# Down projection as seven block products on one Trainium2 core

## Chip, cores and metric

The kernel runs on one core of one Trainium2 chip, as one program. The metric is the device time of one execution in microseconds (us). Three runs of the kernel before took 3605.74, 3605.95 and 3608.25 us; the median is 3605.95 us.

## What is computed

The reference is a two-block model on a sequence of 2048 tokens and 1024 channels, all in float32. The first block is a state space and pooling mixer followed by a gated feed-forward; the second is banded attention beside a gated linear attention, an output product and a second gate. The part that matters here is the feed-forward of the first block:

```
n2 = rmsnorm(h, norm2_g)
ff = silu(n2 @ w_gate) * (n2 @ w_up)      # 1024 -> 2816 columns
h  = h + ff @ w_down                      # 2816 -> 1024 columns
out = rmsnorm(h, final_norm_g)
```

After it a layer norm feeds the second block. 2816 columns are 22 groups of 128 (NFF), 1024 channels are 8 groups of 128 (KT).

## The kernel before, in words

All float32 products run on TensorE as three products of rounded parts. A number x is split into hi (ScalarE copies it to the rounded type float32r, L54) and lo (x minus hi, on VectorE or GpSimd, L44); then hi*hi, hi*lo and lo*hi are summed in PSUM (`mm3`, L163 to L165). A tile is 128 channels x 512 tokens, so a matmul is 128x128 weights against 128x512 values.

The engines have short names in the profile: PE (TensorE), DVE (VectorE), ACT (ScalarE), POOL (GpSimd), SP (its queue issues all loads; ACT's queue issues all stores). Each engine runs its instructions in a fixed order. The program is written for a tile framework that orders the instructions of all engines ahead of time by a simulated timeline: an instruction that stands early in the text has priority, but one that stands later can go ahead when its inputs are simulated to be ready. A generator `self.bg` holds background work (`bg_step`, L892), which only sets where that work stands in the text.

Tokens come in two halves of 1024, and a half in two blocks of 512. For each half there is a gate stage (`gu_half`, L1082) and a down stage (`down`, L1190).

*Gate stage.* For each j of 22 it makes gate and up products for 128 columns of ff and both token blocks. It does so already by seven block products (Winograd's form of Strassen's scheme): gate and up are the two row blocks, the two token blocks the column blocks, and the two halves of the 1024 inputs the inner blocks. A product is 4 x 3 matmuls, so a j has 84. The sums of the inputs are made once per half (`gu_in`, L983), the sums of the weights for each j (`gu_w`, L1037) with the splits on ACT, DVE and POOL. The results h0 and h1 (one per token block) are split by `put` (L1104) into a hi and a lo tile, hid, and stored to memory (`hid_d`), 512 KB each.

*Down stage.* For each token block the 22 hid tiles are loaded again and multiplied with the 22 weight groups of w_down: per j eight output groups m of three matmuls, all eight PSUM banks in use. The weights are loaded and split (ACT, then POOL) anew for each token block through the ring of `get_w`, 88 times in all. After the last j of a block the eight banks are added to h (DVE, L51), the squares and the weighted sum for the next norms are accumulated on ACT, POOL and DVE, and the result is stored (first half) or kept (second half). While down runs in the first half, `gu_in(1)` prepares the second half's inputs; in the second half `proj_in_steps` (L1240) prepares the next stage's. While the gate stage of the second half runs, `norm(0)` and `norm(1)` (L1251) work on the first half's results.

Names that the change and the prediction touch: `weights` (L112), `mix_out` (L953), `gu_w`, `gu_prime` (L1076), `gu_half`, `put`, `slot` (L1156), `fetch` (L1172), `down`, `norm`, `load_x` (L1350). Tiles by name: wr (raw weights), wh and wl (their hi and lo), wru, wsh, wsl, wth, wtl (further gate weight tiles), xh and xl (inputs), raw, t, s, sq, nh, ls (128x512 work tiles), pa, pb, pc (PSUM banks of the gate stage), dn (those of the down stage). A line in the profile can be that of a helper: L44 is every tensor_tensor, L51 every scalar_tensor_tensor, L54 every ScalarE function, L57 a load and L60 a store.

Of the kernel before, what the change touches and what calls it, by code (L numbers as in the profile page):

```python
# [6 lines left out]
F32 = mybir.dt.float32  # L7
F32R = mybir.dt.float32r
# [5 lines left out]
D = 1024  # L14
# [21 lines left out]
class Build:  # L36
# [75 lines left out]
    def weights(self, stage):  # L112
# [7 lines left out]
        for _ in range(2):  # L120
            for j in range(NFF):
                yield a["w_down"][j], sh, None, None
        if stage == "down0":
            return
        for _ in range(2):
# [51 lines left out]
    def run(self):  # L177
        tc, a = self.tc, self.a
        with ExitStack() as ctx:
            dram = ctx.enter_context(tc.tile_pool(name="dram", bufs=1, space=bass.MemoryType.DRAM))  # L180
            for name, shape, dt in (("u_d", [4, T, 128, NCH], F32), ("yp_d", [512, S], F32), ("ys_d", [4, T, 128, NCR], F32),
                                    ("h1_d", [D, S], F32), ("h2_d", [D, S], F32), ("r2_d", [4, 512], F32), ("ryp_d", [1, S], F32), ("rys_d", [T, NCR], F32),
                                    ("h3_d", [D, S], F32), ("hid_d", [4, NFF, 128, 2, 512], F32),
# [610 lines left out]
    def phase_main(self):  # L794
# [4 lines left out]
        with ExitStack() as ctx:  # L799
# [11 lines left out]
            with tc.tile_pool(name="ffn", bufs=1) as self.fp:  # L811
                self.xr.append(self.fp)
                with tc.tile_pool(name="psf", bufs=8, space=PSUM) as self.ps:
# [16 lines left out]
                    for half in range(2):  # L830
                        self.bg = [self.norm(0), self.norm(1)] if half else [self.bias_table()]
# [8 lines left out]
                    self.bg = [self.norm(2), self.norm(3)]  # L840
# [112 lines left out]
    def mix_out(self, bs, start=(), steps=range(8), last=False):  # L953
        a = self.a
        before, self.r2_todo = self.r2_todo, []
        ss = [self.fp.tile([128, 512], F32, tag="hid" if bs[0] else "st2", name="ss", bufs=2) for _ in bs]
# [26 lines left out]
    def gu_in(self, half):  # L983
# [9 lines left out]
        def fetch(k):  # L993
            out = []
            for n, (kk, i) in enumerate(((k, 0), (k, 1), (k + 4, 0), (k + 4, 1))):
                t0 = half * 1024 + i * 512
                f = self.tmp("s", 2) if n % 2 else self.fp.tile([128, 512], F32, tag="nh", name="nh", bufs=2)
# [39 lines left out]
    def gu_w(self, j):  # L1037


        rg, ru = self.gu_raws  # L1040
        w = self.gw = {}
# [11 lines left out]
        if j + 1 < NFF:  # L1053
            self.gu_raws = [self.gu_load(j + 1, up) for up in (False, True)]
# [21 lines left out]
    def gu_prime(self):  # L1076

        self.gu_raws = [self.gu_load(0, False), None]
        self.gw_steps = self.gu_w(0)
        next(self.gw_steps)  # L1080

    def gu_half(self, half):  # L1082
# [21 lines left out]
        def put(i, h):  # L1104
            x = self.fp.tile([128, 2, 512], F32R, tag="hid", name="hid", bufs=2)
            self.split(x[:, 0], x[:, 1], h)
            self.store(self.hid_d[2 * half + i, j], x.bitcast(F32))

        for j in range(NFF):
            w = self.gw  # L1110
            nw = self.gu_w(j + 1) if j + 1 < NFF else iter(())
# [9 lines left out]
            if j == NFF - 1:  # L1121
                self.w_all = self.weights(f"down{half}")
                self.w_next.append(self.get_w(0))
                self.down_start(half)
                self.fetch()
                self.fetch()
# [14 lines left out]
            if j == NFF - 1:  # L1141
                self.fetch()
                self.fetch()
            self.tt(h1, h1, p5, ALU.mult)
            put(1, h1)
# [5 lines left out]
            self.tt(h0, pa, h0, ALU.mult)  # L1151
            put(0, h0)
# [802 lines left out]
```

## Time and profile before

| | |
|---|---|
| median of three runs | 3605.95 us |
| the profiled execution's own time | 3604.71 us |
| its span, first to last instruction | 3602.7 us |
| mean granted TensorE clock | 0.963 of full speed |
| first gate stage begins | 680 us |
| first down stage begins | 1117 us |
| second gate stage begins | 1386 us |
| second down stage begins, ends | 1843, 2086 us |

The stages overlap a little, since the ordering lets instructions of the next stage run early; the borders are those of the first or last matmul of a stage, within a few us. "Busy" is the time in which an engine had at least one instruction running; matmuls overlap, so a busy PE says that it did not stand still, and the distance between starts says how fast it went. PEclk is the granted clock, 1.00 being 2.4 GHz. An instruction's duration on DVE or POOL contains waits for a place in memory that the two share, if there are any.

### The profile page before, as it was taken

The page shows a single profiled execution, that of the slowest core. Times are in us where ns is not written, and L with a number is a line of the kernel's source. Part 1 is how long each engine was busy: PE and PEld are TensorE (multiplying, and loading weights), DVE is VectorE, ACT ScalarE, POOL GpSimd, SP SyncE. Part 2 cuts the span into 40 slices and gives each one's busy share as a digit, 9 for nine tenths or more (in the row PEclk, how much of TensorE's full clock was granted, in tenths as well). Part 3 has the DMA queues.
Part 4 walks back from the last instruction along what each step waited for, and adds up shares of the span by engine and source line. Part 5 has one row for each costly group of instructions (what it writes and reads, how often), then busy time and mean ns, then how long its engine had stood idle before and what let it go on. Part 6 is the DMA issues. An engine that isn't in the chain of part 4 may idle for free.

```text
span 3602.7 us, 45654 instructions
## 1 busy us (share of the span) xinstructions
PE 3326.9 (92%) x16138; PEld 2761.8 (77%) x16138; DVE 2092.3 (58%) x3365; ACT 1565.5 (43%) x2750; POOL 1569.8 (44%) x1146
## 2 busy tenths in 40 slices
PE   7887788899999999999999989999999999979897
PEld 7676666678887877777777877798888987767676
DVE  7776556766667015777642073235666446787874
ACT  5343533334344223445332132335655445666653
POOL 1265544444454455555445453222322235353544
PEclk9998899899999999999999999999999999989898
DMA  9643376442335564444366535665564665555351
GB/s 252 143 108 102 87 227 189 138 141 100 112 117 187 186 237 152 144 167 157 115 234 208 191 124 172 172 185 173 158 185 135 171 194 148 163 141 159 115 170 49
DMA packets 330268, 568.10 MB, mean 158 GB/s; under 512 B 85004, under 2 KB 171556, under 8 KB 330040
## 3 DMA queue, kind: packets, MB, share of 16 engines
q1 hardware_dynamic: 226944, 419.21, 39.6%
q10 hardware_dynamic: 103096, 145.97, 11.7%
q8 instruction: 128, 2.10, 0.2%
q14 instruction: 100, 0.82, 0.1%
HBM read 409.04 MB, written 145.94 MB: 154 GB/s over the span
## 4 chain that ended last, share of the span: by engine, by line
PE 36%; DVE 7%; DMA 5%; ACT 3%; issue 2%; POOL 1%; SPq 0%; ACTq 0%; DVEq 0%; POOLq 0%
PE pt L165 4%; PE pt L163 4%; PE pt L164 4%; PE pa L1092 3%; PE dn L163 2%; PE dn L164 2%; PE dn L165 2%; PE pv L1562 2%; PE s L1520 1%; PE pv L1391 1%; PE pv L1392 1%; PE pc L1092 1%; PE pv L1390 1%; PE tp L1546 1%; DMA raw<-mix_d 1%
## 5 line engine op out<-in xcount | busy, mean ns | idle before, releaser
L44 POOL TENSOR_TENSOR wl<-wr,wh 128x1024 fp32r<-128x1024 f32 (+1 forms) x235 | 587.2, 2500 | 564.4 <-ACT wh L54 512.0
L54 ACT ACTIVATE wh<-wr 128x1024 fp32r<-128x1024 f32 (+2 forms) x289 | 301.4, 1046 | 497.3 <-PE dn L164 275.7
L163 PE MATMUL pt<-xh,wh 128*128 128x512 f32 x896 | 358.8, 401 | 8.7 <-DVE t L51 4.2
L165 PE MATMUL pt<-xh,wl 128*128 128x512 f32 x896 | 358.2, 400 | 2.1 <-POOL wl L44 1.7
L164 PE MATMUL pt<-xl,wh 128*128 128x512 f32 x896 | 357.7, 399 | 0.0
L163 PE MATMUL dn<-hin,wh 128*128 128x512 f32 x704 | 281.8, 400 | 10.7 <-ACT wh L54 7.5
L164 PE MATMUL dn<-hin,wh 128*128 128x512 f32 x704 | 279.7, 397 | 0.0
L48 POOL TENSOR_SCALAR P<-P,rsm 128x640 f32<-128x640 f32 (+4 forms) x128 | 103.8, 811 | 348.3 <-DVE rsm L1530 285.5
L1092 PE MATMUL pa<-xh,wh 128*128 128x512 f32 x528 | 211.7, 401 | 14.3 <-ACT t L54 9.3
L165 PE MATMUL dn<-hin,wl 128*128 128x512 f32 x704 | 215.3, 394 | 0.0
L1092 PE MATMUL pa<-xh,wl 128*128 128x512 f32 x528 | 207.9, 400 | 2.1 <-POOL wl L44 2.1
L1092 PE MATMUL pa<-xl,wh 128*128 128x512 f32 x528 | 209.8, 397 | 0.0
L44 POOL TENSOR_TENSOR wl<-wru,wh 128x1024 fp32r<-128x1024 f32 x44 | 107.6, 2446 | 234.2 <-ACT wh L54 234.1
L163 PEld LDWEIGHTS pt<-xh,wh 128*128 128x128 f32 x896 | 170.0, 190 | 46.1 <-issue 3.9
L44 POOL TENSOR_TENSOR hid<-raw,hid 128x512 fp32r<-128x512 f32 x88 | 126.8, 1453 | 165.3 <-issue 121.7
L165 PEld LDWEIGHTS pt<-xh,wl 128*128 128x128 f32 x896 | 169.0, 189 | 38.0 <-POOL wl L44 2.4
L164 PEld LDWEIGHTS pt<-xl,wh 128*128 128x128 f32 x896 | 169.3, 189 | 35.0 <-issue 0.7
L51 DVE SCALAR_TENSOR_TENSOR h<-dn,h 128x512 f32<-128x512 f32 x32 | 19.8, 678 | 267.2 <-PE dn L165 182.3
L163 PEld LDWEIGHTS dn<-hin,wh 128*128 128x128 f32 x704 | 134.2, 191 | 46.4 <-ACT wh L54 10.9
L1525 DVE CUSTOM_DVE_ANT_0 P<-s,bias 128x640 f32<-128x640 f32 (+4 forms) x128 | 94.5, 738 | 108.5 <-PE s L1520 59.9
L164 PEld LDWEIGHTS dn<-hin,wh 128*128 128x128 f32 x704 | 134.3, 191 | 29.9
L1390 PE MATMUL pv<-wh,xh 128*128 128x256 f32 (+1 forms) x512 | 148.7, 294 | 8.8 <-ACT wh L54 5.4
(474 smaller groups left out, 9345.8 us busy)
## 6 DMA issues: line engine op xcount, KB each, us to landing
hid_d<-hid ACTq DMA_DIRECT2D x88, 512.0 KB, 3.5
wr<-in_w_down SPq DMA_DIRECT2D x88, 512.0 KB, 3.5
hin<-hid_d SPq DMA_DIRECT2D x88, 512.0 KB, 4.2
wr<-in_w_out SPq DMA_DIRECT2D x56, 512.0 KB, 4.3
wr<-in_w_in SPq DMA_DIRECT2D x44, 512.0 KB, 4.5
wru<-in_w_up SPq DMA_DIRECT2D x44, 512.0 KB, 3.7
wr<-in_w_gate SPq DMA_DIRECT2D x44, 512.0 KB, 3.5
raw<-h_d SPq DMA_DIRECT2D x64, 256.0 KB, 4.0
```

The costliest lines, as they stand in the source:

```text
L44: return (eng or self.dve).tensor_tensor(out=o, in0=x, in1=y, op=op)
L48: (eng or self.dve).tensor_scalar(out=o, in0=x, scalar1=s1, scalar2=s2, op0=op0, **kw)
L54: return self.act.activation(out=o, in_=x, func=func, **kw)
L163: self.pe.matmul(ps, lhsT=hi[k], rhs=xh[k], start=(first and k == 0), stop=False)
L164: self.pe.matmul(ps, lhsT=hi[k], rhs=xl[k], start=False, stop=False)
L165: self.pe.matmul(ps, lhsT=lo[k], rhs=xh[k], start=False, stop=(last and k == n - 1))
L1092: self.pe.matmul(ps, lhsT=l_[:, k], rhs=x[k][r_], start=(first and k == n == 0), stop=(k == 3 and n == 2), skip_group_check=True)
L1390: self.pe.matmul(pt, lhsT=xh, rhs=whi[:, k % 4], start=(k == 0), stop=False)
L1391: self.pe.matmul(pt, lhsT=xh, rhs=wlo[:, k % 4], start=False, stop=False)
L1392: self.pe.matmul(pt, lhsT=xl, rhs=whi[:, k % 4], start=False, stop=(k == KT - 1))
L1525: self.dve.tensor_tensor_reduce(out=v3(P[:, 0:w]), in0=sp[:, 0:np_, 0:n], in1=v3(bias[:, 640 - w:640]), scale=1.0, scalar=3e38, op0=ALU.ad ...
L1562: self.pe.matmul(pv, lhsT=VH[:, kb + x - kt0], rhs=self.PT[m][ch][:, sl], start=(n == 0 and m == 0), stop=(n == len(idxs) - 1 and m == 1))
```

## The change

The down product is made by seven block products too. The 22 groups of ff are taken in two halves of 11 (inner blocks: j and j + 11), the 8 output groups in two halves of four, and the two token blocks of a half are the column blocks. So that j and j + 11 come one after the other, the gate stage goes through the groups in the order 0, 11, 1, 12, ... (`gu_js`). It stores h0 and h1 as they are, and with them three more tiles made of sums on POOL: seven tiles of 256 KB for each pair (`hd_d`). The down weights' four sums (128x512 for each of 11 j) are made once by POOL in the first gate stage, in 44 steps of four operations on 128x128 (`down_sums`, two steps per j), and stored (`sd_d`).

The down stage then has 7 products x 11 j = 77 steps per half. A step loads a 128x512 weight tile and a 128x512 ff tile (`dn_load`), splits both on ACT and DVE (`dn_split`, the subtraction by the default engine of `halves`, DVE), and runs 4 m x 3 matmuls into four banks. The products alternate between two sets of four banks (pa, pb). Some results are copied to SBUF (`hold`); outputs are finished four at a time after products 2, 7, 3 and 4, one per step. `dn_load` runs five steps ahead of the matmuls, `dn_split` two; a step's split tiles come in three sets. Other edits move tiles to other tags (places in memory), and the two norms of a half change their order. Weights of the next stages are requested in step 75 of 77.

```diff
@@ gu_w
+        nxt = self.gu_js[j + 1:j + 2]
+        j = self.gu_js[j]
...
@@ gu_half
-        def put(i, h):
-            x = self.fp.tile([128, 2, 512], F32R, tag="hid", name="hid", bufs=2)
-            self.split(x[:, 0], x[:, 1], h)
-            self.store(self.hid_d[2 * half + i, j], x.bitcast(F32))
+        def keep(name):
+            return self.fp.tile([128, 512], F32, tag=name, name=name, bufs=1)
+        def less(o, x, y):
+            self.tt(o, x, y, ALU.subtract, eng=self.pool)
+        def put(p, x):
+            self.store(self.hd_d[half, p - 1, jj], x)
+        sums = iter(()) if half else self.down_sums()
         for j in range(NFF):
+            jj, late = j // 2, j % 2
             w = self.gw
+            next(sums, None)
...
-            self.tt(h1, h1, p5, ALU.mult)
-            put(1, h1)
+            if late:
+                self.tt(h1, h1, p5, ALU.mult)
+                put(3, h1)
+                less(hb, h1, hb)
+                put(7, hb)
+                less(hc, h1, hc)
+                put(6, hc)
+            else:
+                hb = keep("hb")
+                self.tt(hb, h1, p5, ALU.mult)
+            next(sums, None)
...
-            self.tt(h0, pa, h0, ALU.mult)
-            put(0, h0)
+            if late:
+                self.tt(h0, pa, h0, ALU.mult)
+                put(2, h0)
+                less(ha, h0, hc)
+                put(4, ha)
+            else:
+                ha, hc = keep("ha"), keep("hc")
+                self.tt(ha, pa, h0, ALU.mult)
+                put(1, ha)
+                less(hc, hb, ha)
+                put(5, hc)
...
+    def down_sums(self):
+        wd, h = self.a["w_down"], NFF // 2
+        def fetch(j, m):
+            t = self.fp.tile([128, 4, 128], F32, tag="ls", name="sd", bufs=3)
+            self.load(t[:, 0:2], wd[j][:, m::4])
+            self.load(t[:, 2:4], wd[j + h][:, m::4])
+            return t
...
+            for o, x, y, op in ((1, 0, 1, ALU.subtract), (3, 3, 1, ALU.subtract), (0, 0, 3, ALU.add), (2, 2, 3, ALU.subtract)):
+                self.tt(t[:, o], t[:, x], t[:, y], op, eng=self.pool)
+            self.store(self.sd_d[:, j, :, m * 128:(m + 1) * 128].rearrange("s p c -> p s c"), t)
+            yield 1
...
+        self.dn = [(p, j) for p in (1, 2, 6, 5, 7, 3, 4) for j in range(NFF // 2)]
...
+    def dn_split(self):
...
+        w, x = self.dn_raw.pop(0)
+        if self.dn_s % 3 == 1:
+            wh, wl, xh, xl = (self.fp.tile([128, 512], F32R, tag=t, name=t, bufs=1) for t in ("wth", "wtl", "hc", "hd"))
+        else:
+            h, l_ = (self.wp.tile([128, 2, 512], F32R, tag=t, name=t, bufs=2) for t in ("wh", "wl"))
+            wh, xh, wl, xl = h[:, 0], h[:, 1], l_[:, 0], l_[:, 1]
+        self.halves((wh, wl), w)
+        self.halves((xh, xl), x)
...
@@ down
+        def out(x):
+            o, i, m = h1.pop(0)
+            self.stt(o, x, 0.5, o, ALU.mult, ALU.add)
...
+            self.add_sq(sq, o, first)
...
+                self.stt(sz, o, gf[:, m:m + 1], sz, ALU.mult, ALU.add)
+            if not half:
+                self.store(self.h3_d[m * 128:(m + 1) * 128, b * 512:(b + 1) * 512], o)
+            fetch()
...
+            if p in (1, 6, 5):
+                self.fn(hold[p][m], ps, AF.Copy)
+            elif p == 4:
+                out(ps)
+            else:
+                x = hold[{2: 1, 7: 5, 3: 6}[p]][m]
+                self.tt(x, ps, x, ALU.add)
+                out(x)
...
+        for n, (p, j) in enumerate(self.dn):
+            self.dn_split()
+            self.dn_load()
+            wh, wl, xh, xl = self.dn_ops.pop(0)
+            ps = pa if p in (1, 6, 7, 4) else pb
+            for m in range(4):
+                c = slice(m * 128, m * 128 + 128)
+                for i, (l_, r_) in enumerate(((wh, xh), (wh, xl), (wl, xh))):
+                    self.pe.matmul(ps[m], lhsT=l_[:, c], rhs=r_, start=(p in (1, 2, 5) and j == i == 0),
+                                   stop=(j == NFF // 2 - 1 and i == 2), skip_group_check=True)
+            if post:
+                done(*post.pop(0))
+            if j == NFF // 2 - 1:
+                post += [(p, m) for m in range(4)]
+            if n % 4 == 1:
+                self.bg_step()
```

## Rows read from the trace of the kernel before

**Rows 1.** The page's first part: busy us (share of the span) and instructions.

```profile
PE 3326.9 (92%) x16138; PEld 2761.8 (77%) x16138; DVE 2092.3 (58%) x3365; ACT 1565.5 (43%) x2750; POOL 1569.8 (44%) x1146
```

**Rows 2.** Busy time by stage: stretch, length, busy us (instructions), PEclk, DMA, GB/s.

```profile
680.00:1117.00 437.00, 425.76 (x1814) 343.63 (x1813) 290.22 (x299) 175.94 (x254) 209.13 (x112) 0.99 0.33 116
1117.00:1386.20 269.20, 259.36 (x1094) 208.18 (x1093) 72.72 (x67) 66.91 (x80) 139.46 (x65) 0.98 0.64 213
1386.20:1843.00 456.80, 443.04 (x1881) 355.79 (x1881) 321.58 (x337) 206.82 (x298) 236.11 (x128) 0.99 0.42 145
1843.00:2086.00 243.00, 240.41 (x1036) 194.80 (x1037) 42.36 (x37) 62.10 (x73) 120.05 (x54) 1.00 0.65 218
```

**Rows 3.** Instructions that write the tile dn: ns min/median/max, first and last start.

```profile
L163 PE MATMUL dn<-hin,wh x704: 388/395/797, 1117.3 to 2085.3; 128*128 128x512 f32 x176
```

**Rows 4.** Timeline of PE in the first gate half: start us, us, instruction.

```profile
859.91 0.40 PE L1092 MATMUL pa<-xh,wth 128*128 128x512 f32 x1
...
871.93 0.39 PE L1092 MATMUL pa<-xl,wh 128*128 128x512 f32 x1
```

**Rows 5.** PE's waits, 680 to 2086 us: total us, times, longest.

```profile
PE dn L163 <- ACT wh L54: 7.5, 6, 2.7
...
PE dn L163 <- ACT sq L54: 3.0, 2, 1.5
```

**Rows 6.** Busy time of PE (matmuls) in three stretches, PEclk, DMA, GB/s.

```profile
800.00:1100.00 300.00, 300.00 (x1301) 1.00 0.31 111
1120.00:1180.00 60.00, 53.40 (x208) 0.91 0.67 223
1200.00:1220.00 20.00, 20.00 (x88) 1.00 0.58 186
```

**Rows 7.** Timeline of PE around one stall; in brackets the idle time before.

```profile
1467.91 0.56 PE L1092 MATMUL pa<-xh,wh 128*128 128x512 f32 x1 [4.71 <-ACT t L54]
...
1471.66 0.40 PE L1092 MATMUL pa<-xh,wh 128*128 128x512 f32 x1
```

**Rows 8.** Instructions that write or read hid, 800 to 1100 us.

```profile
L54 ACT ACTIVATE hid<-raw x31: 615/616/634, 800.1 to 1091.7; 128x512 fp32r<-128x512 f32 x31
L44 POOL TENSOR_TENSOR hid<-raw,hid x31: 1278/1297/1767, 802.6 to 1095.0; 128x512 fp32r<-128x512 f32 x31
L60 ACTq DMA_DIRECT2D hid_d<-hid x31: 326/326/327, 804.0 to 1096.7; - x31
```

**Rows 9.** Groups of POOL instructions by form: count, busy us, mean ns, idle before.

```profile
L44 POOL TENSOR_TENSOR ed<-Lc 128x256 f32<-128x256 f32 x16 | 11.6, 723 | 55.8 <-DVE Lc L1659 55.8
...
L44 POOL TENSOR_TENSOR vsq<-vsq 128x128 f32<-128x128 f32 x16 | 9.4, 588 | 0.4
```

**Rows 10.** Timeline of POOL in the first gate half.

```profile
858.47 2.40 POOL L44 TENSOR_TENSOR wl<-wru,wh 128x1024 fp32r<-128x1024 f32 x1 [10.02 <-ACT wh L54]
...
863.80 2.40 POOL L44 TENSOR_TENSOR wl<-wr,wh 128x1024 fp32r<-128x1024 f32 x1
```

**Rows 11.** Timeline of DVE in the first gate half.

```profile
859.71 0.69 DVE L44 TENSOR_TENSOR t<-pb,t 128x512 f32<-128x512 f32 x1 [1.46 <-PE pb L1092]
...
864.03 2.72 DVE L44 TENSOR_TENSOR wtl<-sq,wth 128x512 fp32r<-128x512 f32 x1 [1.34 <-ACT wth L54]
...
868.97 0.68 DVE L44 TENSOR_TENSOR sq<-wru 128x512 f32<-128x512 f32 x1
...
872.53 1.23 DVE L44 TENSOR_TENSOR wsl<-wr,wsh 128x1024 fp32r<-128x1024 f32 x1 [0.17 <-ACT wsh L54]
```

**Rows 12.** Timeline of ACT in the first gate half.

```profile
876.74 1.06 ACT L54 ACTIVATE wh<-wru 128x1024 fp32r<-128x1024 f32 x1 [0.99 <-PE pa L1092]
...
877.71 0.63 ACT L54 ACTIVATE hid<-raw 128x512 fp32r<-128x512 f32 x1
```

**Rows 13.** Groups of DVE instructions by form in the first down half.

```profile
L51 DVE SCALAR_TENSOR_TENSOR s<-h,v_final_norm_g,s 128x512 f32<-128x512 f32 x7 | 12.8, 1832 | 0.2
```

**Rows 14.** Busy time in the first 100 us.

```profile
0.00:100.00 100.00, 78.36 (x426) 75.07 (x426) 79.31 (x330) 50.14 (x92) 17.65 (x43) 0.93 0.91 240
```

More of the change, by code (lines that the diff above doesn't have):

```diff
@@ new lines, in down, with fetch @@
+        for _ in range(3):
+            self.dn_load()
+        self.dn_split()
+        pb, pa = ([self.ps.tile([128, 512], F32, tag="ps", name=n, bufs=8) for _ in range(4)] for n in ("pb", "pa"))
+        outs = [(i, m) for i, m0 in ((0, 0), (1, 4), (1, 0), (0, 4)) for m in range(m0, m0 + 4)]
+        h1, kept, sums, hold, post = [], [[None] * KT for _ in range(2)], {}, {}, []
+        def fetch():
+            if outs:
+                i, m = outs.pop(0)
+                if half:
+                    t = kept[i][m] = self.fp.tile([128, 512], F32, tag="x", name="h3", bufs=20)
+                else:
+                    t = self.fp.tile([128, 512], F32, tag=("ha", "hb")[m % 2], name="h3", bufs=1)
+                b = 2 * half + i
+                self.load(t, self.h1_d[m * 128:(m + 1) * 128, b * 512:(b + 1) * 512])
+                h1.append((t, i, m))
@@ new lines, in out @@
+        def out(x):
+            o, i, m = h1.pop(0)
+            b = 2 * half + i
+            self.stt(o, x, 0.5, o, ALU.mult, ALU.add)
+            first = i not in sums
+            if first:
+                sums[i] = [self.tmp("s", 2) if i else self.fp.tile([128, 512], F32, tag="st2", name="st2", bufs=2)
+                           for _ in range(2)]
+            sq, sz = sums[i]
+            self.add_sq(sq, o, first)
+            if first:
+                self.ts(sz, o, gf[:, m:m + 1], ALU.mult)
+            else:
+                self.stt(sz, o, gf[:, m:m + 1], sz, ALU.mult, ALU.add)
+            if not half:
+                self.store(self.h3_d[m * 128:(m + 1) * 128, b * 512:(b + 1) * 512], o)
+            fetch()
@@ new lines, in places, with done @@
+        def places(p):
+            two = [self.fp.tile([128, 2, 512], F32, tag=t, name="hold", bufs=n)
+                   for t, n in ((("wsh", 1), ("wsl", 1)) if p == 5 else (("wru", 2), ("wru", 2)))]
+            hold[p] = [t[:, e] for t in two for e in range(2)]
+        def done(p, m):
+            ps = (pa if p in (1, 6, 7, 4) else pb)[m]
+            if p in (1, 6, 5):
+                if m == 0:
+                    places(p)
+                self.fn(hold[p][m], ps, AF.Copy)
+            elif p == 4:
+                out(ps)
+            else:
+                x = hold[{2: 1, 7: 5, 3: 6}[p]][m]
+                self.tt(x, ps, x, ALU.add)
+                out(x)
@@ new lines, in down @@
+        for _ in range(2):
+            fetch()
+        for n, (p, j) in enumerate(self.dn):
+            self.dn_split()
+            self.dn_load()
+            wh, wl, xh, xl = self.dn_ops.pop(0)
[11 more added lines that the diff above has]
+                self.bg_step()
+            if n == 75:
+                if half:
+                    self.w_all = self.weights("proj")
+                    self.w_next.append(self.get_w(0))
+                else:
+                    self.gu_prime()
+                    next(self.gw_steps)
@@ L1236, in down @@
+        while post:
+            done(*post.pop(0))
+        self.stats = [(*sums[i], kept[i] if half else []) for i in range(2)]
         if half == 0:
@@ L1267, in tiles @@
             return out
-        for _ in range(3 if b % 2 == 0 else 0):
+        if b % 2:
             yield 1
```

123 lines of the change are left out of this document (40 added, 83 removed).

## The prediction

> **What bounds the kernel now.** I read the page's first part, then busy time by stage, then the down products' own instructions, then PE's waits and 20 us stretches. TensorE is busy 92% of the span [rows 1]. The four stages that the change touches run from 680 to 2086 us, and PE is busy for 425.8 of 437.0, 259.4 of 269.2, 443.0 of 456.8 and 240.4 of 243.0 us there [rows 2]: PE sets the time, and 37 us of idle time stand against it. The reader should see that DVE, ACT and POOL have room in the two down stages (DVE 73 of 269 and 42 of 243 us), less in the gate stages.
>
> The down products are 3 x 704 = 2112 matmuls [rows 3]. One lasts 0.39 us, but they are pipelined, so their price is the distance of starts: 53 starts in a row lie between 859.91 and 871.93 us, so 12.02 / 52 = 0.231 us each [rows 4]. 2112 x 0.231 = 488 us.
>
> Of the idle time, 7.5 us is PE waiting for the down weights' rounding and 3.0 us (two waits) for the square that stands before the release of a bank where one token block's down ends and the next begins [rows 5]. The first costs more than its waits: 208 matmuls run from 1120 to 1180 us where 60 / 0.231 = 260 would fit (1301 do in 300 us of the gate stage), so 52 x 0.231 = 12 us are lost at the start of the first down [rows 6]. A stall also lowers the clock: after a wait of 4.71 us the next nine matmuls take from 1467.91 to 1471.66 us, 3.75 instead of 2.08 us, half the pace [rows 7]. So such a stall costs 4.7 + 1.7 = 6.4 us.
>
> **The change, part by part.** *Matmuls.* A half now takes 7 block products x 11 j x 4 m x 3 = 924 matmuls instead of 1056; over both halves 264 fewer, 264 x 0.231 = 61.0 us, all on PE, the bounding engine: -61.0.
>
> *Gate stage, both halves.* Per j two ScalarE roundings of hid go (0.616 each) and two POOL subtractions stay in number (1.297 each, now between h tiles). ACT-queue stores go from 2 to 3.5 per j at 0.326 us of ACT [rows 8]: ACT gains 1.23 and pays 0.49 us. DVE's count is the same. In the first gate half the two sums stores add 0.65. Taken as 0; ends -3 and +5, since a store now waits at the head of ACT's queue for POOL's subtraction, as it does today for hid.
>
> *Weight sums, first gate half.* 44 steps of four POOL operations on 128x128. The one row of that form means 588 ns; going down from 1.297 us at 512 columns [rows 8] and 0.723 at 256 gives 0.44 [rows 9]. So 176 operations add 77 to 103 us of POOL. Each step also puts two loads on SP's queue (prefetched a step ahead) and a store on ACT's, ahead of the next gate weights and copies.
> POOL alone has room (209 of 437 us, rows 2), but it hinders DVE. A DVE subtraction from two SBUF tiles that starts 0.23 us into a 2.40 us POOL operation lasts 2.72 us, ending 0.55 us after it; one that reads PSUM lasts 0.69 beside the same POOL form [rows 10, 11]. So POOL and DVE's two-SBUF operations take turns. Per j that is on POOL 2 x 2.40 + 3 x 1.30 = 8.7 us and on DVE seven of 0.68 and one of 1.23, 6.0 us [rows 11]: 14.7 of the 84 x 0.231 = 19.4 us that PE takes. With eight sums it is 18.2 to 19.4. If nothing overlapped at all, DVE's four PSUM reads included (2.8 us), it would be 21.0 to 22.2, so 22 x 1.6 to 2.8 = 35 to 62 us late. Lower end 0: in the middle of this stage PE is busy for 300.0 of 300 us [rows 6]. Nearest row for a value: the second gate half has 27.0 us more POOL time than the first and 13.8 instead of 11.2 us of PE idle [rows 2]. 90 / 27.0 x 2.6 = 8.7; I take +8.
> The Trainium skill (SBUF — State Buffer, section "Who interferes with whom") says that a DVE instruction with both inputs in SBUF and a GpSimd one that reads SBUF exclude each other for the whole instruction, and one with a PSUM input does not join in; the rows agree (2.72 against 0.69 us). By it alone the demand just fits, the term is 0 and the sum 8 us lower; it speaks against the place of the sums, not against the change.
>
> *Down stage, splits.* Before, ACT rounds the weights (1.06 for such a tile) and POOL subtracts (2.40) once per 24 matmuls [rows 10, 12], and hid comes split from memory. Now each of the 154 steps of 12 matmuls (12 x 0.231 = 2.77 us) has two ACT roundings (1.23 us) and two DVE subtractions (2 x 0.68 = 1.36 us). Both run beside PE: 44% and 49% of a step. A split's operands come free three steps ahead, so it has two steps, 5.55 us, for a chain of about 0.62 + 0.62 + 0.68 and hand-overs, some 2.6 us: slack 2.9 us. Cost 0 in the steady state. Without this cover, PE would wait for the whole excess of each step.
>
> *Down stage, outputs.* Evacuations are now spread: copies to SBUF after products 1, 6 and 5 (a ScalarE pass as hid's, about 0.62, four each), and four outputs, one per step, after products 2, 7 and 3; the last four come after product 4. The old block switch and its 3.0 us go: -3. An output is a sum, two more DVE operations and a POOL addition. The accumulation of the normalisation's sum means 1.832 us where POOL adds the squares, against 0.68 unhindered [rows 11, 13]. In turns: splits 1.36 + two of 0.68 + 1.30 = 4.0 us against a step of 2.77: 1.25 late per step, 5.0 in four, less the slack of 2.9: 2.1 us of stall, in six bursts (three in each half). Ends: 0 (the order lets the splits go first) and 6 x (4.0 + 1.7) = 34 with the clock's fall. I take 6 x 2 = +12.
>
> *Starts and ends of the down stages.* Step 1's operand lands in the tile hc, which is free only after the last gate product, a DVE multiplication (0.69), a POOL subtraction (1.30) and its store: its split ends 3.5 us or so after the gate stage, PE needs it after 2.77. +1 per half, +2; ends 0 and +14. The background work of the first down (13 DVE operations for each of 4 k, as before) still meets its first steps, so I leave the 12 us lost there as they are; ends -11 and +11. At the end four outputs instead of eight are left, but the next gate's third weight tile must wait for the last step, which uses its place: 0, ends -5 and +5.
>
> *Transfers.* 512 KB per 12 matmuls is as many bytes per matmul as now (512 KB of weights and 512 KB of hid per 24): 524 KB / 2.77 us = 189 GB/s. The down stages move 213 and 218 GB/s at a share of 0.64 and 0.65 [rows 2]. Rows of a transfer get half as long. Five steps are loaded ahead. The nearest stretch with shorter rows moves 240 GB/s at a share of 0.91 [rows 14]; by that the down would need a share of 0.72. Taken as 0. Upper end: part of the six bursts' end above, since a load that is late stops the same split.
>
> **Sum.** The profiled execution took 3604.7 us (span 3602.7 and 2.0 around it). 3604.7 - 61.0 + 8 - 3 + 12 + 2 = 3562.7. The median before is 3605.95, 1.2 above, so 3564.
>
> **Rivals.** (a) Nothing new stalls: the order of the work absorbs sums and bursts, 3606 - 61 - 3 = 3542. For it: the 300 us without a wait. Against it: each of the four stages has some idle time already. (b) The outputs' bursts and late loads stall each time and pull the clock down: 3564 + (34 - 12) = 3586. For it: the 1.832 us; against: only 4 of 11 steps have outputs. (c) Slower: ACT's queue. A sums store stands in ACT's order until POOL's four operations end; behind it stands the copy of pa, without which PE may not add product 6 into that bank. If POOL is late by its turns with DVE, PE stalls as at 1467.91 (6.4 us). Once in every j of the first gate half this is 22 x 6.4 = 141, so 3564 + 141 = 3705. Alone it turns the gain of 42 us into a loss from 42 / 6.4 = 7 such stalls; once in two j gives 3564 + 70 = 3634. For it: that very wait is the one of [rows 7]. Against: ACT's order does not follow the program text in the trace: the rounding of wru runs at 876.74 us, ahead of hid's at 877.71 that stands before it in the text [rows 12]; so a waiting store is placed late; and today's stores wait for POOL in the same way at little cost. (d) The products are not fewer in time: no, 264 matmuls less can't fail to show on PE's count.
>
> **How the numbers follow.** Forecast (3550 to 3580) 0.53, (a) 0.16, (b) 0.16, (c) 0.12, and 0.03 for an even outcome. The range reaches to (a) and past (b) to the even outcome: 3540 to 3606, leaving about 0.15 to 0.2 out. About 0.2% (7 us) can be told from no change here: faster (under 3599) 0.83, same 0.05, slower 0.12.
>
> **What would show it.** Down matmuls 1848, and PE busy less by 264 of them; the two down stages about 30 us shorter each. In the first gate half POOL about 80 to 100 us busier, DVE's two-SBUF means longer, PE idle 8 us more. In the down, PE waits for xl, wl or xh in steps 22 to 26, 55 to 59 and 66 to 70 of each half. Wrong: PE waits for the copy of pa in most j (case c), or no waits at output bursts (case a).

## The result, and the profile after

The changed kernel takes 3578.76 us (median; 3573.63 to 3588.34 in 4 runs) where the kernel before took 3605.84 beside it: a ratio of 0.9927 [0.9904, 0.9951], some 27 us less. The forecast was 3564, 42 us less, with a range of 3540 to 3606. So sign and range held, and a third of the gain is missing. The profiled execution is the longest of the four, 3588.3 us (span 3586.4), 16.4 less than the 3604.7 before. One execution of e2_nosums (4700 us) and one of e7_normsp (9742 us), further down, took far longer than the others of the same kernel and are left out of the medians.

The page's first part answers [rows 1]: 16138 - 15874 = 264 matmuls fewer, as stated, and PE busy 53.1 us less.

```profile
PE 3273.8 (91%) x15874; PEld 2712.4 (76%) x15874; DVE 2253.7 (63%) x3697; ACT 1608.9 (45%) x2906; POOL 1469.1 (41%) x1234
```

The four stages of [rows 2], cut at the first matmul of each (columns as there; the last gate products still run beside the first down step):

```profile
679.20:1135.20 456.00, 431.19 (x1816) 342.80 (x1815) 267.16 (x294) 150.28 (x209) 302.56 (x271) 0.98 0.46 149
1135.20:1376.80 241.60, 225.12 (x961) 183.30 (x960) 168.97 (x242) 116.05 (x205) 46.43 (x23) 0.96 0.69 221
1376.80:1840.90 464.10, 435.94 (x1825) 347.58 (x1824) 314.00 (x334) 182.17 (x255) 230.46 (x124) 0.97 0.40 135
1840.90:2077.70 236.80, 224.18 (x960) 181.69 (x959) 144.81 (x208) 110.50 (x193) 23.24 (x15) 0.97 0.62 198
```

The first gate stage got 18.7 us longer than [rows 2] has it (437.3 from 680.0 to 1117.3), with POOL busy 302.6 instead of 209.1 us. The down stages lost matmuls, but not the 30 us each that 132 fewer should give: from first down matmul to the end, 268.9 became 241.6 and 255.7 (before, from 1829.6 us) became 236.8. PE is idle for 16 and 13 us in them.

What PE waited for, from 680 to 2086 us, answers [rows 5]:

```profile
PE pa L1091 <- ACT t L54: 28.8, 16, 7.9
PE pa L1316 <- ACT hc L54: 20.2, 2, 10.3
PE pa L1091 <- ACT wth L54: 6.7, 1, 6.7
PE pb L1316 <- DVE hd L44: 5.3, 2, 4.3
PE pa L1091 <- DVE wtl L44: 3.8, 1, 3.8
...
PE pc L1091 <- ACT wsh L54: 3.2, 1, 3.2
```

Four things are to be seen there, and each was followed to its place.

*The sums came early.* All instructions on the tile of the weight sums (ns min/median/max, first and last start):

```profile
L44 POOL TENSOR_TENSOR sd<-sd x176: 446/464/1457, 653.5 to 890.0; 128x128 f32<-128x128 f32 x176
...
L60 ACTq DMA_DIRECT2D sd_d<-sd x44: 366/377/711, 657.4 to 890.5; - x44
```

The text asks for two of the 44 steps per j over 22 j, to 1135 us. They ran from 653 to 890 us, in half that time. PE's pace in three stretches (busy us, matmuls, PEclk, DMA, GB/s) shows the price: 797 matmuls from 680 to 900 us, where the kernel before ran 875, and where the pace of [rows 6] (1301 in 300 us) would give 954:

```profile
680.00:900.00 220.00, 195.19 (x797) 0.95 0.66 203
900.00:1140.00 240.00, 240.00 (x1039) 1.00 0.29 101
1225.00:1376.00 151.00, 151.00 (x665) 1.00 0.73 236
```

In the first stretch the stall of rival (c) happened, with the shape that the prediction gave it. The timeline of all engines around the longest wait:

```profile
763.67 2.55 POOL L44 TENSOR_TENSOR sd<-sd 128x128 f32<-128x128 f32 x5
...
765.84 0.38 ACTq L60 DMA_DIRECT2D sd_d<-sd  x1
766.57 0.75 DVE L51 SCALAR_TENSOR_TENSOR nh<-nh,v_norm_g,r 128x512 f32<-128x512 f32 x1 [2.31 <-DMA nh<-h_d]
768.89 0.75 DVE L51 SCALAR_TENSOR_TENSOR nh<-nh,v_norm_g,r 128x512 f32<-128x512 f32 x1 [1.57 <-DMA nh<-h_d]
769.37 1.40 POOL L44 TENSOR_TENSOR sd<-sd 128x128 f32<-128x128 f32 x3 [3.15 <-DMA sd<-in_w_down]
769.56 0.69 DVE L44 TENSOR_TENSOR ha<-pa,raw 128x512 f32<-128x512 f32 x1
770.27 0.34 ACTq L60 DMA_DIRECT2D hd_d<-ha  x1
...
770.80 0.37 ACTq L60 DMA_DIRECT2D sd_d<-sd  x1
771.27 0.63 ACT L54 ACTIVATE wth<-sq 128x512 fp32r<-128x512 f32 x1 [8.58 <-DMA sd_d<-sd]
...
771.81 0.58 ACT L54 ACTIVATE t<-pa 128x512 f32<-128x512 f32 x1
...
772.44 0.80 PE L1091 MATMUL pa<-xh,wh 128*128 128x512 f32 x1 [7.87 <-ACT t L54]
```

ACT does nothing for 8.58 us, from 762.69 us on, and the copy of pa (tile t) behind is what PE wants. Three stores stand at ACT's head in turn. A sums store waits for POOL's sums until 765.84. The store of the gate output ha then waits until 770.27 for DVE, which writes ha at 769.56 and had stood waiting for loads of nh. A second sums store goes at 770.80. So the sums' stores hold ACT for some 3.3 us of the 8.58 and the gate output's store for 4. Such a wait is long only once: of the nine waits for t, 14.1 us in all, one has 7.9 and one 2.5, and the others have 1.1 or less.

*The output bursts cost nothing.* The third stretch above holds all three bursts of the first down half, from 1228 to 1364 us, and PE has no gap in it. The engines do take turns there, as a pair of one burst shows in the timeline:

```profile
1321.66 2.00 POOL L44 TENSOR_TENSOR s<-s,sq 128x512 f32<-128x512 f32 x1 [79.26 <-ACT sq L54]
...
1322.43 1.79 DVE L51 SCALAR_TENSOR_TENSOR s<-h,v_final_norm_g,s 128x512 f32<-128x512 f32 x1
```

The splits are simply not delayed by more than their slack. In the second half PE waits 2.7 us in all between 1880 and 2078 us.

*Each down half starts late.* PE waits 10.31 us in its second step (and 9.93 at 1862 us). The timeline around the tile hc, from the last gate matmul on:

```profile
1146.01 0.40 PE L1091 MATMUL pa<-xh,wl 128*128 128x512 f32 x1
...
1146.59 1.27 POOL L44 TENSOR_TENSOR hb<-raw,hb 128x512 f32<-128x512 f32 x1 [14.37 <-issue]
...
1147.81 1.71 POOL L44 TENSOR_TENSOR hc<-raw,hc 128x512 f32<-128x512 f32 x1
...
1150.89 0.33 ACTq L60 DMA_DIRECT2D hd_d<-hc  x1
...
1156.04 0.63 ACT L54 ACTIVATE hc<-s 128x512 fp32r<-128x512 f32 x1 [0.75 <-DMA hd_d<-hc]
...
1156.72 0.79 PE L1316 MATMUL pa<-hc,wth 128*128 128x512 f32 x1 [10.31 <-ACT hc L54]
```

POOL's result of 1149.5 is stored from 1150.89 on, and the tile is free 5 us later, when the store has landed. Only then may step 1's operand be rounded into it. Most stores of this tile land sooner, and these two land while the DMA engines are full. The landing of all its stores, then the two stretches from issue to reuse (1st and 2nd half; columns as in [rows 2]):

```profile
DMA to landing us min/median/max: 2.0/2.3/5.7
...
1150.89:1156.04 5.15, 0.00 (x0) 0.00 (x0) 5.12 (x7) 3.42 (x6) 2.53 (x3) 0.54 0.99 331
1856.53:1861.41 4.88, 0.00 (x0) 0.00 (x0) 3.28 (x5) 1.77 (x3) 1.15 (x1) 0.50 0.99 322
```

The mean DMA share of the two stages is 0.69 and 0.62. That the full engines make the landing long fits, but no run tests it.

*The second gate half starts late.* The timeline around its third weight tile, wth:

```profile
1379.32 2.03 SPq L57 DMA_DIRECT2D h<-h_d  x2
...
1382.42 0.69 DVE L51 SCALAR_TENSOR_TENSOR h<-pa,h 128x512 f32<-128x512 f32 x1 [1.47 <-DMA h<-h_d]
...
1383.16 5.96 POOL L44 TENSOR_TENSOR st<-st,sq 128x512 f32<-128x512 f32 x4
...
1387.93 1.74 DVE L44 TENSOR_TENSOR sq<-wru 128x512 f32<-128x512 f32 x1
...
1389.70 0.63 ACT L54 ACTIVATE wth<-sq 128x512 fp32r<-128x512 f32 x1 [1.80 <-DVE sq L44]
...
1390.39 0.80 PE L1091 MATMUL pa<-xh,wth 128*128 128x512 f32 x1 [6.73 <-ACT wth L54]
```

The DVE subtraction that wth is rounded from (sq<-wru) stands behind the last outputs, and these wait for their loads.

### The profile page after: what moved, and what is told of

Same layout as the page of the kernel before. It is cut to its first block, busy times and chain, and to the rows that moved or that the text cites. A ratio compares the mean times of both kernels' runs of the same rounds, so it can differ in the third digit from the quotient of the medians.

```text
span 3586.4 us, 46677 instructions
## 1 busy us (share of the span) xinstructions
PE 3273.8 (91%) x15874; PEld 2712.4 (76%) x15874; DVE 2253.7 (63%) x3697; ACT 1608.9 (45%) x2906; POOL 1469.1 (41%) x1234
## 5 line engine op out<-in xcount | busy, mean ns | idle before, releaser
L44 POOL TENSOR_TENSOR wl<-wr,wh 128x1024 fp32r<-128x1024 f32 (+1 forms) x147 | 372.7, 2537 | 314.7 <-ACT wh L54 295.2
L54 ACT ACTIVATE wh<-wr 128x1024 fp32r<-128x1024 f32 (+3 forms) x303 | 272.7, 902 | 341.6 <-PE pt L159 75.8
L44 DVE TENSOR_TENSOR wl<-wr,wh 128x512 fp32r<-128x512 f32 (+2 forms) x156 | 150.3, 964 | 106.0 <-ACT wh L54 105.6
L44 POOL TENSOR_TENSOR s<-s,sq 128x512 f32<-128x512 f32 x56 | 87.9, 1569 | 285.6 <-ACT sq L54 284.4
L1489 PE MATMUL pv<-wl,xh 128*128 128x256 f32 (+1 forms) x512 | 147.6, 289 | 0.7 <-POOL wl L44 0.7
L1490 PE MATMUL pv<-wh,xl 128*128 128x256 f32 (+1 forms) x512 | 147.0, 288 | 0.0
L1091 PE MATMUL pc<-xh,wsh 128*128 128x512 f32 x352 | 139.1, 395 | 6.0 <-ACT wsh L54 3.2
L1091 PEld LDWEIGHTS pa<-xh,wh 128*128 128x128 f32 x528 | 101.5, 192 | 54.2 <-ACT t L54 24.6
L54 ACT ACTIVATE wsh<-wr 128x1024 fp32r<-128x1024 f32 x44 | 46.6, 1060 | 211.9 <-PE pc L1091 149.8
L1091 PE MATMUL pc<-xl,wsh 128*128 128x512 f32 x352 | 139.0, 395 | 0.0
```

What stands on the lines that cost most here:

```text
L44: return (eng or self.dve).tensor_tensor(out=o, in0=x, in1=y, op=op)
L54: return self.act.activation(out=o, in_=x, func=func, **kw)
L1091: self.pe.matmul(ps, lhsT=l_[:, k], rhs=x[k][r_], start=(first and k == n == 0), stop=(k == 3 and n == 2), skip_group_check=True)
L1489: self.pe.matmul(pt, lhsT=xh, rhs=wlo[:, k % 4], start=False, stop=False)
L1490: self.pe.matmul(pt, lhsT=xl, rhs=whi[:, k % 4], start=False, stop=(k == KT - 1))
```

## The experiments

All are timed against the kernel before on the same chip (medians there 3606.97, 3607.59, 3610.1 and 3605.76 us in four groups: e1 to e4, e5 to e8, e9 to e11, e12). As these differ by up to 4.3 us, versions of different groups are best compared by their ratios. Since one profiled execution stands behind each trace, this table gives the same three lengths from each (us, worked out from the first gate matmul of each half and the last down matmul): A, first gate and down half; B, second gate and down half; rest, to the end of the span.

```
run              start    A      B      rest     median   ratio to before
before           680.0  706.2  699.1  1517.4    3605.84
changed          679.2  697.6  700.9  1508.7    3578.76   0.9927 [0.9904, 0.9951]
e1_paced         680.6  685.8  693.7  1516.4    3578.50   0.9917 [0.9903, 0.9930]
e2_nosums        680.5  675.9  695.6  1512.5    3566.22   0.9889 [0.9875, 0.9904]
e3_step1         687.2  688.1  685.3  1503.5    3566.50   0.9886 [0.9871, 0.9900]
e4_spstore       683.8  706.8  698.3  1508.3    3591.89   0.9957 [0.9945, 0.9969]
e5_paced_step1   681.4  685.2  684.4  1515.8    3567.36   0.9886 [0.9870, 0.9901]
e6_tail          690.5  696.1  692.8  1502.3    3586.19   0.9942 [0.9929, 0.9954]
e8_all           683.8  686.5  679.4  1504.9    3559.91   0.9875 [0.9858, 0.9892]
e9_wth           685.9  684.2  675.2  1513.8    3562.08   0.9872 [0.9851, 0.9894]
e10_noless2      685.5  692.8  679.8  1514.1    3571.75   0.9894 [0.9877, 0.9911]
e11_normlate     684.5  693.5  690.4  1508.2    3578.44   0.9913 [0.9898, 0.9929]
e12_best         682.6  688.9  671.5  1510.4    3552.33   0.9852 [0.9835, 0.9868]
```

The columns start and rest are of work that no edit touches, and they vary by 11 and 15 us among these executions. So a difference of a few us in the whole is read from medians with intervals, and one of a stage from its trace.

**e1_paced: the sums held back.**

```
+            self.anchor = self.tt(o, x, y, ALU.subtract, eng=self.pool)   # in less(), and likewise for ru in gu_w
...
+            with self.tc.issue_after(self.anchor.ins):
+                for o, x, y, op in (...): self.tt(t[:, o], t[:, x], t[:, y], op, eng=self.pool)
```

> The four POOL operations of each weight-sum step are tied behind POOL's latest gate instruction in the text, so that they run in the j that they stand in (two steps per j over 22 j) and not all in the first eleven. Theory A (the loss in the first gate half comes from the sums being packed: 176 operations between 653 and 890 us): the 18 us that the stretch 680 to 900 lost against the kernel before come back for the most part; matmuls in 680 to 900 rise from 797 towards 875, sums last until about 1100 us, time 8 to 18 us below the changed kernel. Rival B (a sums step costs the same wherever it runs, by turns of POOL and DVE): the loss moves into 900 to 1140 us, time within 5 us.

The sums now run from 671 to 1149 us, and PE's pace is even (waits for t 6.1 instead of 14.1 us in the stage):

```profile
L44 POOL TENSOR_TENSOR sd<-sd x176: 447/466/1482, 671.2 to 1149.1; 128x128 f32<-128x128 f32 x176
```

```profile
680.00:900.00 220.00, 207.95 (x867) 0.97 0.50 156
900.00:1140.00 240.00, 235.76 (x1001) 1.00 0.48 149
```

A is 11.8 us shorter, but the median did not move (3578.5 against 3578.8), which is rival B's number. Part of the loss moved, too: 70 matmuls more run before 900 us and 38 fewer from there to 1140. Other versions repeat the stage: from the first gate matmul to the first down matmul, the five traces with the sums held back (e1, e5, e8, e9, e12) take 445.9 to 448.8 us and five with the sums early (changed, e3, e6, e10, e11) 452.4 to 456.0, and the longest wait for t is 2.8 to 3.2 instead of 6.6 to 8.7 us. So the place of the sums is shown for the stage, at some 7 us; its worth in the whole is not resolved.

**e2_nosums: no sums at all** (`sums = iter(())`, and the four sum products read a plain weight tile).

> Leaves the weight sums out: no loads, POOL operations or stores for them; the four products that use a sum get a plain slice of w_down in its place (the output is not the reference's). All theories: this bounds what the sums cost. A and B both say 15 to 20 us below the changed kernel, with 680 to 900 us back at about 870 matmuls. If the gate outputs' own edits (3.5 instead of 2 stores, POOL subtractions) are what costs, it stays within 5 us.

3566.2 us, and A 675.9 against 697.6: all of the sums cost 21.7 us in the trace and 12.5 in the median, less than the 15 to 20 expected, though the pace came back (879 matmuls from 680 to 900 us). Of the 21.7, e1 gives 11.8 to their early place; the 9.9 left are the sums themselves, spread. The medians divide it otherwise: 0.3 for the place and 12.3 for the spread sums (e1 against e2). The waits for hc (10.3 and 11.4 us), for wth and wsh, and the second gate half's 14.0 us for t are all still there, so none of them comes from the sums.

**e3_step1: step 1's operand in another tile.**

```
-            wh, wl, xh, xl = (... for t in ("wth", "wtl", "hc", "hd"))
+            if self.dn_s == 1:
+                xh, xl = (self.fp.tile([128, 512], F32R, tag="ls", name=t, bufs=3) for t in ("hc", "hd"))
...
```

> Only the second step of each down half puts its ff split into two places of the tag ls instead of hc and hd. Theory C (that step waits for the store of hc to land): PE's two waits of 10.3 and 9.9 us for hc go, and with them the half-speed stretch behind each; 15 to 24 us below the changed kernel. Rival D (the first steps are late anyway, by loads that wait in SP's queue and by DVE's background work): the waits move to the next steps' wh, wl or xh, time 0 to 6 us below.

3566.5 us, 12 less than the changed kernel; A 9.5 and B 15.6 shorter. PE's waits at the two starts, 1120 to 1230 and 1820 to 1900 us:

```profile
PE pa L1320 <- DVE wl L44: 4.8, 2, 3.4
PE pb L1320 <- DVE hd L44: 1.9, 1, 1.9
PE pb L1320 <- DVE wl L44: 1.7, 2, 0.9
...
PE pa L1320 <- DVE wl L44: 2.3, 2, 2.1
PE pa L1320 <- ACT hc L54: 0.2, 1, 0.2
```

The cause is shown: 20.2 us of waits for hc become 0.2. The 25.1 us of A and B are not all from it, since some 7 of them lie in the two gate halves, which the edit doesn't touch. From the first down matmul on, the halves are 8.7 and 9.6 us shorter. The second repeats in every trace: 236.0 to 238.1 us in the six that keep this tile (changed, e1, e2, e4, e6, e11), 226.4 to 227.7 in the five with the other tile (e3, e5, e8, e9, e12), and 227.1 in e10, where no store of hc stands ahead of the second down. In the first half, part of it (8 us) comes back as waits for DVE's splits, which share DVE with the next gate's operands, the loss that [rows 6] showed before.

**e4_spstore: the sums' stores on SP's queue** (`self.store` to `self.load` for that one transfer).

> Only the stores of the weight sums are issued by SP's queue instead of ACT's. Theory E (what stops PE in the first gate half is ACT's queue: a sums store at its head waits for POOL, the copy of pa stands behind it): PE's waits for ACT's t between 680 and 900 us (14 us in the changed kernel) fall under 5, time 8 to 15 us below. Rival F (POOL and DVE taking turns is what delays): the waits stay, or move to wtl and wl, time within 4 us; it could also be slower, if the waiting stores hold up loads on SP.

3591.89 us, ratio 0.9957 [0.9945, 0.9969]: 13 us slower than the changed kernel at the medians, with intervals that just overlap, and A is 9.2 us longer. PE's waits from 680 to 1140 us:

```profile
PE pa L1091 <- ACT wh L54: 8.0, 3, 3.5
PE pa L1091 <- ACT t L54: 6.4, 4, 3.3
```

The waits for t halve (14.1 in the changed kernel), so the sums' stores on ACT's queue held about half of them, but PE now waits for wh, the rounding of loaded weights: SP stands 72.7 us for POOL's sums in this stage (3.9 in the changed kernel), with the weights' loads behind. That wh is late by it is read from the order of the loads and not tested.

**e5_paced_step1: both edits.**

> Both edits together: the sums' POOL operations kept behind the gate stage's own, and step 1's operand in another tile. Theory A (the sums' early rush on POOL costs its own time in the gate stage, whatever the start of down costs): the two add up; alone they gave 0 and -12 us at the medians, and the paced gate stage was 9 us shorter in its trace, so by the trace 3566.5 - 5 to 9 = 3558 to 3562. Rival (PE time won in the gate stage comes back as a wait elsewhere, as with the pacing alone): 3564 to 3570. In the trace: waits for hc below 0.5 us in both starts, waits for t in the first gate half about 5 us instead of 14.

3567.4 us: the rival's number. A and B together are 3.8 us shorter than with step 1's tile alone, and the median is not. The gate stage is shorter (446.5 us to the first down matmul, e3 455.1), but the first down half is longer (238.7 against 233.0, no shorter than the 238.7 of e1), with PE waiting for DVE's splits where it had waited for hc.

**e6_tail: more tiles for the last outputs' loads.**

```
+                if p == 7 and m == 3 and not half:
+                    tags.extend([dict(tag="ls", bufs=3)] * 3)   # beside ("ha", 1), ("hb", 1)
+                    place[0] = 2
+                    for _ in range(3):
+                        fetch()
```

> Only the tiles for the last outputs of the first down half change: from the end of product 7 on, the loads of h1 go round five tiles instead of two, three more ahead. Theory T (the gate that follows waits 6.7 us for wth and 3.2 for wsh because the last two outputs' loads are issued only at 1379 us, when the first two stores have freed their tiles, and DVE and POOL end the outputs 4 us late): the loads are there before product 4 ends, the two waits fall to 0 to 5 us together, the stage is 5 to 9 us shorter, time 3578.8 - 5 to 9 = 3570 to 3574. Rival (the waits come from POOL's four additions of squares, 5.96 us in a row, and from the third weight tile that the last step holds, not from the loads): the waits stay over 7 us together, time 3576 to 3580.

3586.2 us, not faster. The waits fall only to the bound of the rival, over 7 us (1380 to 1420 us):

```profile
PE pa L1091 <- ACT wth L54: 4.4, 1, 4.4
PE pc L1091 <- ACT wsh L54: 2.8, 1, 2.8
```

So the outputs' loads are the smaller part of it: the two waits lose 2.7 of 9.9 us, and 47 matmuls instead of 32 run in the half's first 20 us. As the main cause, theory T is dropped. Why this kernel is above the changed one in time, while A and B are shorter in its trace, isn't settled.

**e7_normsp: the normalisation's stores on SP's queue** (both stores of the first two blocks).

> The stores of the first two blocks' normalisation, done beside the second gate half, go on SP's queue instead of ACT's. Theory N (PE's 14 us of waits for the copy of pa there, 6.4 before the change, come from those stores: they stand at the head of ACT while DVE's nh waits for POOL): the waits for t in 1400 to 1835 us fall to 5 to 8 us, time 3578.8 - 5 to 9 = 3570 to 3574. Rival 1 (they come from the normalisation's ACT and DVE operations themselves, which wait for loads of nh and for POOL): the waits stay at 12 to 15 us, time 3576 to 3581. Rival 2 (as with the sums' stores, a store at the head of SP's queue holds up the weights' loads behind it): waits for wh and wth grow, time 3582 to 3592.

3579.7 us, 0.9922 [0.9908, 0.9935]: rival 1's time, and theory N's did not come. Its waits can't be read beside the others, and a stage's gain need not show in the time (e1), so theory N is not borne out, but not refuted either.

**e8_all: e5 and e6 together.**

> The three edits that keep the computation: sums paced, step 1's operand in another tile, five tiles for the last outputs. If the stalls are separate losses (theories A, C and T together): 3558 to 3562 less 5 to 9, so 3550 to 3556. If what is won at one place comes back at the next (rival): no better than step 1's tile alone, 3562 to 3570. The forecast's sum with its +12 for the outputs' bursts taken out is 3552.

3559.9 us, between both expectations, and A and B add to 1365.9 against 1369.6 of e5. The intervals of e5 and e8 overlap, and with e6 alone slower, the tail's tiles are not shown to help.

**e9_wth: the third gate weight ahead of the outputs** (on e5, without e6).

```
+            if self.dn_s == 76 and not self.dn_half:
+                wh, wl = (self.fp.tile([128, 512], F32R, tag="ls", name=t, bufs=3) for t in ("wth", "wtl"))
...
                     self.gu_prime()
                     next(self.gw_steps)
+                    next(self.gw_steps)
```

> Made on the version with paced sums and step 1's own tile (3567.4 us): the last step of the first down half gets other tiles for its weights, so that wth is free earlier, and the next gate's third weight tile is made one step of the text earlier, ahead of the last outputs. Theory W (PE's waits for wth, 6.8 us, and wsh, 3.2 to 4.8, at the start of the second gate half come from the weight step being queued behind the outputs on DVE, not from the outputs' loads): both waits together fall from 10 to 11.6 us to 0 to 4, the first 20 us of that half have 55 to 75 matmuls instead of 32, time 3567.4 - 6 to 9 = 3558 to 3561. Rival (the outputs, now later, hold the banks that the gate needs): a new wait for h on DVE takes over, time 3564 to 3570.

3562.1 us; B 675.2 against 684.4 of e5, nearly all of it in the gate half (470.5 to 461.8 us from its first to its last matmul), 67 matmuls in its first 20 us instead of 32. PE's waits at the start, 1360 to 1400 us:

```profile
PE pa L1091 <- POOL wl L44: 2.2, 1, 2.2
PE pc L1091 <- ACT wsh L54: 0.3, 1, 0.3
```

Theory W is shown for the stage: the order on DVE, with the loads the smaller part (e6). The kernel before ran 63 matmuls in these first 20 us, so the start is back to what it was. In time it is 5 us, with overlapping intervals.

**e10_noless2: no subtractions of gate outputs in the second half.**

```
-                less(hb, h1, hb); put(7, hb); less(hc, h1, hc); put(6, hc)
+                if not half: ...   # and the same for products 4 and 5
```

> Output not the reference's: in the second gate half the four POOL subtractions of gate outputs per pair of j and the stores of their results are left out; products 6, 5, 7 and 4 of the second down read another tile of the same size. All else is the changed kernel. Theory G (the second gate half is some 19 us longer than before because of these 44 subtractions and stores, which I had costed at 0): from the gate's first to its last matmul 475 us fall to 458 to 463, the waits for t from 14 to 5 to 8 us, time 3578.8 - 12 to 17 = 3562 to 3567. Rival (its start and the normalisation beside it do it): 470 to 475 us, waits for t 11 to 15, time 3575 to 3581 less 0 to 4 for the missing wait for the store of hc at the second down's start, which goes here in any case, up to 10; so 3565 to 3579, and the stage's length decides.

3571.8 us. The gate half takes 466.7 us instead of 475.0, and its waits for t fall (1400 to 1830 us):

```profile
PE pa L1091 <- ACT t L54: 2.9, 3, 1.3
```

That is neither number: 8.3 us of the stage, half of what theory G said, and the late start of the gate half stays. The untouched versions e1, e2, e3 and e6 have 468.0 to 471.4 us there, so the subtractions and stores cost 1 to 8 us here; I put them at some 4.

**e11_normlate: the normalisation three steps late**, as before the change.

```
-        if b % 2:
+        for _ in range((1 if kept else 3) if b % 2 else 0):
             yield 1
```

> Changed kernel, but the normalisation beside the second gate half starts three steps of the background late, as before the change, instead of one. Theory B (the normalisation now meets the end of the outputs and the catching up of the gate's weights, so its start is what makes the second gate half longer): the gate's 475 us fall by 4 to 8, time 3571 to 3576. Rival (it collides with the gate's own operations wherever it lies): 472 to 478 us and 3576 to 3581.

The gate half falls to 464.3 us, more than expected, and the time stays at 3578.4 (ratio 0.9913 [0.9898, 0.9929] against 0.9927): each theory has one of its numbers, so alone it decides nothing.

**e12_best: e9 and e11 together.**

> Paced sums, step 1's own tile, the third gate weight ahead of the last outputs, and the normalisation three steps late: the edits that shortened their own stage in a trace, together. If the stage times add up (461.8 us of second gate half with the weight step alone, and 4 to 10 less with the late normalisation): 452 to 458 us there and 3562 - 4 to 8 = 3554 to 3558. Rival (time won beside the normalisation does not show in the whole, as with the late normalisation alone, 3578.4 against 3578.8 us): 3560 to 3565.

3552.3 us, 0.9852 [0.9835, 0.9868], better than both expectations, and the fastest version here. Its second gate half is 457.7 us, as the first theory had it, and 455.6 before the change: with all its subtractions in it, it is 2 us longer than before, so its start and the normalisation beside it made most of what it had lost. The interval lies below the changed kernel's; against e9 (0.9851 to 0.9894) it overlaps.

## Why the prediction was right, and where its sizes were wrong

*Matmuls, -61.0.* Held: 264 fewer. The down matmuls also run a little closer than the 0.231 us of [rows 4]: 663 start between 1225 and 1376 us, 0.228 us apart.

*Weight sums, +8.* The term was mis-sized, at 21.7 in the trace and 12.5 in the medians (e2). The price for sums spread over the stage was about right, 9.9 in the trace and 12.3 in the medians (e2 against e1). What failed for the stage is the premise that they would be spread "eight sums" per j: they were queued ahead as soon as their loads let them, into half the stage. I had used the fact that order on an engine does not follow the text as an argument against rival (c); it was the argument for it. By the Trainium skill (SBUF — State Buffer, section "Who interferes with whom") alone the term was 0. No run contradicts that rule, but e4 shows that the order on ACT's queue, and not only the engines' turns, was part of the cost. What the spread sums' 10 to 12 us come from, turns or something else, no run separates.

*Outputs, -3 + 12.* The bursts cost 0 in the first half and at most 2.7 us in the second, the lower end of that term, as rival (a) had it. The turns are there (1.79 beside 2.00 us), but the accumulation of a burst is not 1.832 every time, it goes down to 0.75, and the slack, estimated at 2.9 us, was enough for the rest.

*Starts of the down, +2 with an upper end of 14.* This is the step that failed most: 18.3 us in the two down halves of e3, of which the 9.6 of the second are won in every trace with the other tile, while the 8.7 of the first are not won where the sums are held back (e5). I let step 1's split end "3.5 us or so after the gate stage". The last gate matmul ends at 1146.4 and the split begins at 1156.0. Two POOL subtractions stand in a row (hb, then hc, to 1149.5), where I had counted one; ACT's queue takes 1.4 us more; and the store takes 5 us from its issue to the tile's release, for which the 3.5 us leave no room. After the stall the matmuls run at half pace until 1161.2 us (granted clock 0.50, the level of 1.2 GHz), some 2 us more, as [rows 7] had it.

*Transition to the second gate half, 0 with ends of 5.* 9.2 us in B (e9). I named the tile that the last step holds, but not that the weight's DVE step would then stand behind the outputs.

*Gate outputs, 0.* Right within what can be told in the first half: without the sums (e2) the gate stage takes 436.3 us to the first down step against 437.3 before. In the second half some 4 us, within the ends (e10); in e12, with all of them in it, the half is 2 us longer than before.

*A term that the prediction lacks.* The normalisation beside the second gate half starts one step of the background late instead of three. Moving it back shortens that half by 4.1 us in e12 against e9, and by 3.7 to 10.7 in e11 against the versions without it; the time of e11 alone shows no gain.

*The sum again.* With terms from the traces, A + B: 1405.3 - 61.0 - 3 + 21.7 + 18.3 + 9.2 + 4 = 1394.5, where the trace has 1398.5. The 4 us left are of the size by which the second gate half of this one trace (475.0) exceeds those of e1, e2, e3 and e6 (468.0 to 471.4). The difference to the forecast of -42 for both is 35 us in this trace, 15 in the medians; the terms for sums, starts and transition were 39 us too low together, and the bursts' 12 too high. That the median lies at the upper edge of the 3550 to 3580 of the forecast is therefore in part luck: the unneeded 12 us set off some of what was missing. Why the traces' losses are larger than the medians' is open. e12, which has the four edits together, has A + B 44.9 us below before, about what the forecast had said of the change.

## What to carry to other kernels

When a tile changes hands through a store, price the landing of the store and the queue that it stands in, not only the operations; a spare tile for one step was worth 11 to 12 us here (e5 against e1, e3). Added work that depends only on its own loads need not stay where the text puts it: price it for the place to which it can run ahead, and look what stands behind its store. The next stage's preparation can end up behind the last outputs of this one, so ask which of the next weights is queued behind the last outputs.

## What the hardware showed that I had not expected

- From the issue of a 128x512 store to the reuse of its tile 5.15 us passed (1150.89 to 1156.04), against 0.33 us of ACT's time, at a DMA share of 0.99; the median landing of this tile's stores is 2.3 us.
- Down matmuls in the changed order run at 0.228 us (663 starts between 1225 and 1376 us), gate matmuls of the same shape at 0.231 [rows 4]. Why is open.
- Three output bursts left PE without a gap at 236 GB/s and a DMA share of 0.73, above the 0.64 and 0.65 of the down stages in [rows 2].
- Nearly the same instructions ahead of the first gate stage took 679 to 690 us in thirteen traces, so one trace's total is no measure of an edit of 10 us.
